# Residual tiles and norm rows loaded several steps ahead of use; a product's sums copied bank by bank in its last step

## The chip, the cores and the metric

One core of a Trainium2 chip runs the whole program. The metric is device time in microseconds (us): the median of several executions of the same program. Engines are named as in the profile: PE is TensorE's matmul, PEld its weight load, DVE is VectorE, ACT is ScalarE, POOL is GpSimd, and SP is SyncE, which here only issues DMAs (SPq is its queue).

## The reference

One layer of a decoder with 1024 tokens and width 1024, in float32. An attention and a retention branch are projected out and normalised to `x1`; then comes a gated MLP with a causal convolution of width 3 (inner width 2816). The change lies in its last lines:

```python
u = causal_depthwise_conv(h @ w_up[l], conv_w[l], conv_b[l])
a, bv = jnp.split(u, 2, axis=-1)
y = (jax.nn.gelu(a, approximate=False) * bv) @ w_down[l]
x = layer_norm(ALPHA * x + g2 * y, ln2_g[l], ln2_b[l])
```

The `x` on the right of the last line is `x1`, the result of the first sub-layer. With `g = gelu(a) * bv` as the matrix of 1024 x 2816, the stage in question computes `g @ w_down`, adds the residual `ALPHA * x1`, and normalises each row.

## The kernel before

The stages follow one another on PE: input projections, attention, retention, output projection, the up product with convolution and gate, and last the down product, on which this document centres (from 1032 us of the profile on).

**The down product** is cut 2 x 2 in each dimension and done with seven products of half size instead of eight, in the order `PORD = (1, 2, 6, 5, 3, 7, 4)` (L1379). The operands of a product `p` are sums of blocks; they lie ready in DRAM (`gd`, `sd`, `td`, and `w_down` itself), and `d_src` (L1262) says which. Each product has `NK` = 11 steps `k` over the inner dimension. A float32 operand is split into a high part `hi` (rounded to the format that PE multiplies in one pass) and the rest `lo`, and a product of two numbers takes three matmuls: hi x hi, hi x lo, lo x hi (`d_mm`, L1291). A step is 4 row tiles `i` x 3 matmuls, 128 x 128 against 128 x 512.

**Sums.** There are two sets of four banks: `X_` (products 1, 6, 7 and 4 add into it, one after the other) and `Z_` (products 2, 5 and 3; product 2 ends with new banks taken for 5). Between products the running sums are needed, so `keep` (L1368) has ACT copy the four banks to SBUF after products 1, 6 and 5 (`s1`, `u2`, `s5`), after the last matmul of all four. After product 5 it copies `Z_`, into which product 3 adds next; after product 1 and 6 it copies `X_`, which the next product does not touch. After product 7 DVE adds `X_` into `s5` (L1446), and product 4 adds into `X_` next. Product 4 runs with the row tile outside and the step inside (L1447): the first bank goes through all 11 steps before the second begins.

**Preparation.** `d_prep` (L1270) makes the operands of one step: two loads of 256 KB into a `raw` tile, issued on SP (L1273); the cast to `hi` on ACT (L1287; for product 6 two halves, L1278 and L1279); the split `lo = raw - hi` on DVE (L1288; product 6: L1280 and L1282). `d_more` (L1384) runs the preparations `AHEAD` = 11 steps before PE's step (L1381, L1409). Tiles come from tagged pools: raw tiles from `R` (4), `hi` and `lo` of even steps from `X` (16), of odd steps from `H` (16), kept tiles and residual tiles 0 to 3 from `VM` (10). A tile is free again when its last reader is done.

**Beside the products** DVE works on the result, one row tile of 128 x 1024 at a time. `finish0(i)` (L1300) takes a tile `acc`, loads `x1` rows into it (L1302), multiplies by the first norm row scaled with ALPHA (L1303) and adds the second (L1304). `result` and `part` (L1322, L1317) add the gated sums; `finish1` and `finish2` (L1334, L1350) normalise and store. `row_load(q)` (L1393) loads one of four norm rows, the same for all partitions, and for q < 2 scales it on ACT at once (L1397). They are called at fixed steps (L1412 to L1427): the two rows at product 2, steps 4 and 6; `finish0` 0 to 3 at product 6, steps 0, 2, 4, 6; 4 and 5 at product 5, steps 2 and 6; 6 and 7 at product 3, steps 2 and 6.

**Order.** Each engine and SP's queue work in order. The order is made when the program is built: instructions are taken by their place in the program, but one that is expected to be ready sooner can go first on its engine. `tc.issue_after(ins)` puts what its block issues on the engine of `ins` behind `ins`, on that engine only. Waits are put in by the framework.

Of the kernel before, what the change touches and what calls it, by code (L numbers as in the profile page):

```python
# [8 lines left out]
F32 = mybir.dt.float32  # L9
# [4 lines left out]
ALU = mybir.AluOpType  # L14
# [17 lines left out]
def kernel(  # L32
# [35 lines left out]
    def slot(tag, shape, dtype, name, padded=None):  # L68
        return gp.tile(shape, dtype, tag=tag, bufs=NB[tag], name=name, padded_shape=padded)
# [4 lines left out]
    def small(shape, name):  # L74
        return sp.tile(shape, F32, tag="s", bufs=24, name=name)

    def f(ap):
        return ap.bitcast(F32)
# [66 lines left out]
    def bcast_rows(src, n):  # L145
        return bass.AP(tensor=src.tensor, offset=src.offset, ap=[[0, P], [1, n]])
# [1112 lines left out]
    nc.sync.dma_start(g_row, bcast_rows(gates[1], D))  # L1259
    dops = {}  # L1260

    def d_src(p, k):  # L1262
        half = [slice(0, 512), slice(512, 1024)]
        a = {1: gd[2 * k, :, half[0]], 2: gd[2 * k + 1, :, half[0]], 3: sd[3, k],
             4: gd[2 * k + 1, :, half[1]], 5: sd[0, k], 6: sd[1, k], 7: sd[2, k]}[p]
        b = {1: wdq[0, k][:, half[0]], 2: wdq[1, k][:, half[0]], 3: wdq[1, k][:, half[1]],
             4: td[3, k], 5: td[0, k], 6: td[1, k], 7: td[2, k]}[p]
        return a, b

    def d_prep(p, k):  # L1270
        raw = slot("R", [P, 2, 512], F32, f"dr{p}_{k}")
        for u, src in enumerate(d_src(p, k)):
            nc.sync.dma_start(raw[:, u, :], src)  # L1273
        tag = "X" if p == 1 and k < 4 else "HX"[k % 2]
        hi = slot(tag, [P, 2, 512], F32R, f"dh{p}_{k}")
        lo = slot(tag, [P, 2, 512], F32R, f"dl{p}_{k}")
        if p == 6:
            nc.scalar.copy(hi[:, 0, :], raw[:, 0, :])  # L1278
            nc.scalar.activation(hi[:, 1, :], raw[:, 1, :], AF.Copy, scale=-1.0)  # L1279
            nc.vector.tensor_tensor(out=lo[:, 0, :], in0=raw[:, 0, :], in1=f(hi[:, 0, :]),  # L1280
                                    op=ALU.subtract)
            nc.vector.scalar_tensor_tensor(  # L1282
                out=lo[:, 1, :], in0=raw[:, 1, :], scalar=-1.0, in1=f(hi[:, 1, :]),
                op0=ALU.mult, op1=ALU.subtract,
            )
        else:
            nc.scalar.copy(hi, raw)  # L1287
            nc.vector.tensor_tensor(out=lo, in0=raw, in1=f(hi), op=ALU.subtract)  # L1288
        dops[p, k] = (hi, lo)

    def d_mm(p, k, i, pt, start, stop):  # L1291
        hi, lo = dops[p, k]
        q = slice(i * P, (i + 1) * P)
        for n_, (w_, m_) in enumerate(((hi, hi), (hi, lo), (lo, hi))):
            nc.tensor.matmul(pt, w_[:, 0, q], m_[:, 1, :], start=start and n_ == 0,  # L1295
                             stop=stop and n_ == 2, skip_group_check=True)

    lrow, fr, fin = [], [], {}

    def finish0(i):  # L1300
        acc = slot("VM" if i < 4 else "H", [P, D], F32, f"r{i}")
        nc.sync.dma_start(acc, x1d[i])  # L1302
        nc.vector.tensor_tensor(out=acc, in0=acc, in1=lrow[0], op=ALU.mult)  # L1303
        nc.vector.tensor_tensor(out=acc, in0=acc, in1=lrow[1], op=ALU.add)  # L1304
        fin[i] = [acc, small([P, 2], f"fsum{i}")]

    def gated(i, n, src, dst):

# [8 lines left out]
    def part(i, n, src):  # L1317
        sl = slice(n * 512, (n + 1) * 512)
        gated(i, n, src, src)
        nc.vector.tensor_tensor(out=fin[i][0][:, sl], in0=fin[i][0][:, sl], in1=src, op=ALU.add)  # L1320

    def result(i, n, src, dst, first):  # L1322

        acc, sums = fin[i]
        sl = slice(n * 512, (n + 1) * 512)
        gated(i, n, src, dst)
        nc.vector.tensor_tensor_reduce(
            out=acc[:, sl], in0=acc[:, sl], in1=dst, scale=1.0,
            scalar=(0.0 if first else sums[:, 0:1]),
            op0=ALU.add, op1=ALU.add,  # L1330
            accum_out=sums[:, 0:1] if first else sums[:, 1:2],
        )
# [32 lines left out]
        if i < NT - 1:  # L1365
            nc.sync.dma_start(out[i * P:(i + 1) * P, :], o)

    def keep(pts, name, tag):  # L1368

        ts = [slot(tag, [P, 2, 512], F32, f"{name}{q}") for q in range(2)]  # L1370
        for i in range(4):
            nc.scalar.copy(ts[i // 2][:, i % 2, :], pts[i])  # L1372
        return [ts[i // 2][:, i % 2, :] for i in range(4)]

    def banks4(name):
        t = [bank2(f"{name}{i}") for i in range(2)]
# [7 lines left out]
    def d_more(n):  # L1384
        nonlocal need
        while need < min(n, len(prep)):
            d_prep(*prep[need])
            need += 1

    def dscr(name):  # L1390
        return tmp([P, 512], F32, name)

    def row_load(q):  # L1393
        r_ = slot("X", [P, D], F32, f"frow{q}")
        nc.sync.dma_start(r_, bcast_rows(ln_rows[q], D))
        if q < 2:
            nc.scalar.activation(r_, r_, AF.Copy, scale=ALPHA)  # L1397
        (lrow, fr)[q // 2].append(r_)

    d_more(4)  # L1400
    X_ = [bank(f"dX{i}") for i in range(4)]
    for pi, p in enumerate(PORD[:-1]):
        on_x = p in (1, 6, 7)
        if p in (2, 5):
            Z_ = banks4(f"dZ{p}_")
        pts = X_ if on_x else Z_
        start, stop = p in (1, 2, 5), p in (2, 3)
        for k in range(NK):
            d_more(pi * NK + k + 1 + AHEAD)  # L1409
            for i in range(4):  # L1410
                d_mm(p, k, i, pts[i], start and k == 0, stop and k == NK - 1)
            if p == 2 and k in (4, 6):  # L1412
                row_load(k // 2 - 2)
            if p == 6 and k in (0, 2, 4, 6):
                finish0(k // 2)
            if p == 5:
                if k in (1, 3, 5, 7):
                    result(k // 2, 0, s1[k // 2], s1[k // 2], True)
                if k in (2, 6):
                    finish0(4 + k // 4)  # L1420
            if p == 3:
                if k in (1, 3, 5, 7):
                    part(k // 2, 1, u2[k // 2])
                if k in (2, 6):
                    finish0(6 + k // 4)
                if k in (4, 8):
                    row_load(1 + k // 4)  # L1427
        if p == 1:
            s1 = keep(X_, "ds1_", "VM")
        elif p == 2:  # L1430
            for i in range(4):
                nc.vector.tensor_tensor(out=s1[i], in0=s1[i], in1=Z_[i], op=ALU.subtract)
        elif p == 6:
            u2 = keep(X_, "du2_", "VM")
        elif p == 5:
            s5 = keep(Z_, "ds5_", "VM")
        elif p == 3:
            for i in range(4):
                result(i, 1, Z_[i], dscr(f"dt{i}"), False)
            for i in range(4):  # L1440
                if i > 0:
                    finish2(i - 1)
                finish1(i)
            finish2(3)
    for i in range(4):
        nc.vector.tensor_tensor(out=s5[i], in0=s5[i], in1=X_[i], op=ALU.add)  # L1446
    for i in range(4):  # L1447
        for k in range(NK):
            d_mm(4, k, i, X_[i], False, k == NK - 1)
# [79 lines left out]
```

## Time and profile before

| | us |
|---|---|
| median of 3 runs | 1264.28 |
| lowest and highest run | 1261.54, 1265.71 |
| the profiled execution | 1270.5 |
| its span, first to last instruction | 1268.8 |
| PE busy in it | 1226.6 |
| DVE, ACT, POOL busy | 928.2, 630.4, 247.9 |
| mean granted clock of TensorE | 0.989 of full speed |

The times of rows are from the profiled execution, counted from the first instruction. The down product begins at 1032 us (its first matmul in the regular sequence at 1035.6) and PE's last matmul ends at 1260.6; from there DVE, ACT and a store take the span to its end. Matmuls overlap, so the distance of their starts tells the pace, not the duration in the row.

### The profile page before, as it was taken

The numbers are of one execution on the slowest core, as the hardware profiler recorded it, in microseconds if no ns is written. First come the engines' busy times: TensorE is split into PE (matmuls) and PEld (weight loads), VectorE is DVE, ScalarE is ACT, GpSimd is POOL, SyncE is SP. The second block draws the span as 40 slices with busy tenths as digits, with TensorE's granted clock in tenths as the row PEclk, the third lists the DMA queues.
The fourth block names the chain that finished last, engine by engine and source line by source line (L and its number), as shares of the span: only waits on it lengthen the run. The fifth ranks groups of instructions, "written<-read, shape, count | busy, mean of one in ns | idle before, by whom it ended". The sixth has DMA issues, their size and how long they took to land.

```text
span 1268.8 us, 17244 instructions
## 1 busy us (share of the span) xinstructions
PE 1226.6 (97%) x6077; PEld 1022.3 (81%) x6077; DVE 928.2 (73%) x1774; ACT 630.4 (50%) x1144; POOL 247.9 (20%) x293
## 2 busy tenths in 40 slices
PE   6999999999999999999899999999999999998997
PEld 5788888898888887788788888888888878886876
DVE  6774685784877778747897787787787785784775
ACT  3633232333766668467764454454454565443342
POOL 0034153410433334300003222221101010000021
PEclk9999999999999999999899999999999999998989
DMA  9534152533234236222248877786544689866641
GB/s 354 206 96 137 52 155 95 168 118 118 84 96 146 76 100 195 90 98 105 79 137 211 216 179 178 199 191 159 157 133 126 181 249 278 298 214 203 209 150 67
DMA packets 86047, 199.79 MB, mean 157 GB/s; under 512 B 9861, under 2 KB 16197, under 8 KB 85961
## 3 DMA queue, kind: packets, MB, share of 16 engines
q1 hardware_dynamic: 73288, 175.62, 40.2%
q0 software_dynamic: 12672, 23.07, 11.6%
q8 instruction: 48, 0.79, 0.2%
q14 instruction: 39, 0.31, 0.1%
HBM read 165.06 MB, written 68.20 MB: 184 GB/s over the span
## 4 chain that ended last, share of the span: by engine, by line
PE 74%; DVE 11%; DMA 7%; ACT 4%; issue 2%; SPq 1%; POOL 0%; DVEq 0%; ACTq 0%; POOLq 0%
PE uX L1123 6%; PE uX L1124 6%; PE uX L1125 6%; PE dX L1295 5%; PE uY L1124 4%; PE uY L1125 4%; PE uY L1123 4%; PE rp L208 3%; PE rp L209 3%; PE rp L207 3%; PE pv L793 3%; DVE dl L1288 2%; PE dZ L1295 2%; DMA xt<-in_xT_dram 2%; PE qk L709 2%
## 5 line engine op out<-in xcount | busy, mean ns | idle before, releaser
L1287 ACT CAST dh<-dr 128x1024 fp32r<-128x1024 f32 x66 | 68.2, 1051 | 97.3 <-DMA dr<-in_w_down_dram 39.0
L1288 DVE TENSOR_TENSOR dl<-dr,dh 128x1024 fp32r<-128x1024 f32 x66 | 80.6, 1236 | 42.5 <-ACT dh L1287 32.7
L755 POOL TENSOR_TENSOR S<-S,dn 128x128 f32<-128x128 f32 (+3 forms) x64 | 74.1, 1162 | 150.4 <-DVE dn L754 97.8
L970 POOL DMA_DIRECT2D sd<-gd x22 | 18.1, 823 | 395.2 <-DMA sd<-y 233.0
L207 PE MATMUL rp<-wr,hhi 128*128 128x512 f32 x200 | 79.2, 396 | 1.3 <-ACT rst L367 1.3
L208 PE MATMUL rp<-wr,hhi 128*128 128x512 f32 x200 | 79.0, 395 | 0.1
L209 PE MATMUL rp<-wr,hlo 128*128 128x512 f32 x200 | 78.8, 394 | 0.0
L1295 PE MATMUL dX<-dh 128*128 128x512 f32 x176 | 69.8, 397 | 3.1 <-DVE ds L1446 3.1
L1295 PE MATMUL dX<-dl,dh 128*128 128x512 f32 x176 | 69.7, 396 | 0.0
L1295 PE MATMUL dX<-dh,dl 128*128 128x512 f32 x176 | 69.5, 395 | 0.0
L1138 ACT COPY u<-uX 128x512 f32<-128x512 f32 x44 | 25.8, 586 | 73.8 <-PE uX L1125 73.8
L1295 PE MATMUL dZ<-dh 128*128 128x512 f32 x132 | 52.8, 400 | 5.9 <-ACT ds L1372 5.9
L751 ACT ACTIVATE S<-S,mn 128x128 f32<-128x128 f32 (+3 forms) x64 | 49.9, 779 | 15.1 <-DVE mn L746 13.9
L709 PE MATMUL qk<-hhi,wqh 128*128 128x512 f32 x128 | 54.6, 426 | 0.0
L784 DVE TENSOR_TENSOR pt<-pt,pt 128x512 fp32r<-128x512 f32 (+2 forms) x96 | 50.8, 550 | 4.3 <-ACT pt L783 3.1
L746 DVE CUSTOM_DVE_ANT_0 S<-ps,nb 128x128 f32<-128x128 f32 (+3 forms) x64 | 47.9, 750 | 8.0 <-PE ps L744 5.6
L1295 PE MATMUL dZ<-dl,dh 128*128 128x512 f32 x132 | 52.4, 397 | 0.0
L1295 PE MATMUL dZ<-dh,dl 128*128 128x512 f32 x132 | 52.3, 398 | 0.0
L793 PE MATMUL pv<-pt,V 128*128 128x256 f32 x320 | 49.9, 293 | 2.4 <-DVE pt L784 1.2
L208 PE MATMUL op<-wol,mxs 128*128 128x512 f32 x128 | 50.4, 394 | 1.7 <-DVE wol L893 1.5
L207 PE MATMUL op<-woh,mxs 128*128 128x512 f32 x128 | 50.7, 398 | 0.9 <-DVE mn L746 0.9
L711 PE MATMUL qk<-hhi,wql 128*128 128x512 f32 x128 | 51.6, 403 | 0.0
(1058 smaller groups left out, 3833.4 us busy)
## 6 DMA issues: line engine op xcount, KB each, us to landing
ada<-in_ada_dram SPq DMA_DIRECT2D x48, 512.0 KB, 3.9
td<-in_w_down_dram SPq DMA_DIRECT2D x44, 256.0 KB, 5.5
wa<-in_w_up_dram SPq DMA_DIRECT2D x22, 512.0 KB, 5.6
wb<-in_w_up_dram SPq DMA_DIRECT2D x22, 512.0 KB, 4.0
gd<-y SPq DMA_DIRECT2D x22, 512.0 KB, 2.7
sd<-y SPq DMA_DIRECT2D x44, 256.0 KB, 3.4
dr<-sd SPq DMA_DIRECT2D x44, 256.0 KB, 4.0
dr<-td SPq DMA_DIRECT2D x44, 256.0 KB, 3.4
```

Of the source, the lines that this page charges most:

```text
L207: nc.tensor.matmul(pt, ahi, whi, start=start, stop=False)
L208: nc.tensor.matmul(pt, ahi, wlo, start=False, stop=False)
L209: nc.tensor.matmul(pt, alo, whi, start=False, stop=stop)
L709: nc.tensor.matmul(pt, whi[:, j, :], hhi[j][:, sl], start=(j == 0), stop=False)
L755: nc.gpsimd.tensor_tensor(out=Ssb[:, :span], in0=Ssb[:, :span], in1=den.to_broadcast([P, span]), op=ALU.mult,)
L793: nc.tensor.matmul(pv[:, :256], V2[h][:, kb, :], pts[kb // 4][u][:, kb % 4, :], start=(kb == 0 and u == 0), stop=(kb == nkb - 1 and u == 1),)
L1123: nc.tensor.matmul(pt, whi, bh, start=start, stop=False, skip_group_check=True)
L1124: nc.tensor.matmul(pt, whi, bl, start=False, stop=False, skip_group_check=True)
L1125: nc.tensor.matmul(pt, wlo, bh, start=False, stop=stop, skip_group_check=True)
L1287: nc.scalar.copy(hi, raw)
L1288: nc.vector.tensor_tensor(out=lo, in0=raw, in1=f(hi), op=ALU.subtract)
L1295: nc.tensor.matmul(pt, w_[:, 0, q], m_[:, 1, :], start=start and n_ == 0, stop=stop and n_ == 2, skip_group_check=True)
```

## The change

`finish0` loses its load, which becomes `rest_load`, called four to seven steps earlier. The first two rows are loaded at product 2, steps 0 and 1, and scaled by a call of its own at steps 6 and 8. `keep` now also issues the matmuls of the last step, one bank at a time, each followed by its copy. In the last three steps of product 5 no preparation is issued; the three follow after the copies, and on ACT behind the last copy. At the end of product 7 each bank's matmuls are followed by its add, and the splits of product 4's last three steps go behind the first add on DVE. The other calls of the table `SIDE` stand at the same steps as before.

```diff
+    LATE = [(4, k) for k in range(NK - 3, NK)]
+    late = []
...
         if p == 6:
             nc.scalar.copy(hi[:, 0, :], raw[:, 0, :])
             nc.scalar.activation(hi[:, 1, :], raw[:, 1, :], AF.Copy, scale=-1.0)
...
         else:
             nc.scalar.copy(hi, raw)
-            nc.vector.tensor_tensor(out=lo, in0=raw, in1=f(hi), op=ALU.subtract)
         dops[p, k] = (hi, lo)
+
+        def low():
...
+            else:
+                nc.vector.tensor_tensor(out=lo, in0=raw, in1=f(hi), op=ALU.subtract)
+
+        if (p, k) in LATE:
+            late.append(low)
+        else:
+            low()
...
-    def finish0(i):
+    def rest_load(i):
         acc = slot("VM" if i < 4 else "H", [P, D], F32, f"r{i}")
         nc.sync.dma_start(acc, x1d[i])
+        fin[i] = [acc, small([P, 2], f"fsum{i}")]
+
+    def finish0(i):
+        acc = fin[i][0]
         nc.vector.tensor_tensor(out=acc, in0=acc, in1=lrow[0], op=ALU.mult)
         nc.vector.tensor_tensor(out=acc, in0=acc, in1=lrow[1], op=ALU.add)
-        fin[i] = [acc, small([P, 2], f"fsum{i}")]
...
-    def keep(pts, name, tag):
-
-        ts = [slot(tag, [P, 2, 512], F32, f"{name}{q}") for q in range(2)]
+    def keep(p, k, pts, name):
+
+        ts = [slot("VM", [P, 2, 512], F32, f"{name}{q}") for q in range(2)]
+        ts = [ts[i // 2][:, i % 2, :] for i in range(4)]
         for i in range(4):
-            nc.scalar.copy(ts[i // 2][:, i % 2, :], pts[i])
-        return [ts[i // 2][:, i % 2, :] for i in range(4)]
+            d_mm(p, k, i, pts[i], False, False)
+            order["ACT"] = nc.scalar.copy(ts[i], pts[i])
+        return ts
...
+    SIDE = {
+        2: {0: [(row_load, 0)], 1: [(row_load, 1)], 3: [(rest_load, 0)], 5: [(rest_load, 1)],
+            7: [(rest_load, 2)], 9: [(rest_load, 3)],
+            6: [(row_scale, 0)], 8: [(row_scale, 1)]},
+        6: {0: [(finish0, 0)], 2: [(finish0, 1)], 4: [(finish0, 2)], 6: [(finish0, 3)],
+            7: [(rest_load, 4)], 9: [(rest_load, 5)]},
+        5: {1: [(first_part, 0)], 2: [(finish0, 4)], 3: [(first_part, 1)],
+            5: [(first_part, 2), (rest_load, 6)], 6: [(finish0, 5)], 7: [(first_part, 3)],
+            8: [(rest_load, 7)]},
+        3: {1: [(second_part, 0)], 2: [(finish0, 6)], 3: [(second_part, 1)],
+            4: [(row_load, 2)], 5: [(second_part, 2)], 6: [(finish0, 7)],
+            7: [(second_part, 3)], 8: [(row_load, 3)]},
+    }
...
         for k in range(NK):
-            d_more(pi * NK + k + 1 + AHEAD)
-            for i in range(4):
-                d_mm(p, k, i, pts[i], start and k == 0, stop and k == NK - 1)
...
+            if not (p == 5 and k >= NK - 3):
+                d_more(pi * NK + k + 1 + AHEAD)
+            if k == NK - 1 and p in (1, 6, 5):
+                kept = keep(p, k, pts, f"ds{p}_")
+            else:
+                for i in range(4):
+                    d_mm(p, k, i, pts[i], start and k == 0, stop and k == NK - 1)
+                    if p == 7 and k == NK - 1:
+                        add = nc.vector.tensor_tensor(
+                            out=s5[i], in0=s5[i], in1=X_[i], op=ALU.add)
+                        if i == 0:
+                            with tc.issue_after(add.ins):
+                                for low in late:
+                                    low()
+            for fn, i in SIDE.get(p, {}).get(k, ()):
+                fn(i)
...
         elif p == 5:
-            s5 = keep(Z_, "ds5_", "VM")
+            s5 = kept
+            with tc.issue_after(order["ACT"].ins):
+                d_more((pi + 1) * NK + AHEAD)
...
-    for i in range(4):
-        nc.vector.tensor_tensor(out=s5[i], in0=s5[i], in1=X_[i], op=ALU.add)
```

`first_part` and `second_part` are the calls of `result` and `part` from before under a name; `row_scale` is the scaling that stood in `row_load`.

## Rows read from the trace of the kernel before

**Rows 1.** The page, engine totals and TensorE's clock in 40 slices.

```profile
PE 1226.6 (97%) x6077; PEld 1022.3 (81%) x6077; DVE 928.2 (73%) x1774; ACT 630.4 (50%) x1144; POOL 247.9 (20%) x293
...
PEclk9999999999999999999899999999999999998989
```

**Rows 2.** Waits of PE, whole span: total us, times, longest.

```profile
PE m L232 <- DMA ada<-in_ada_dram: 7.5, 1, 7.5
PE dZ L1295 <- ACT ds L1372: 5.9, 2, 3.9
PE dX L1295 <- DVE ds L1446: 3.1, 1, 3.1
```

**Rows 3.** Table by stretches: us, busy PE PEld DVE ACT POOL, clock, DMA share, GB/s.

```profile
1065.30:1095.20 29.90, 29.90 (x133) 24.77 (x132) 17.10 (x24) 18.80 (x31) 0.00 (x0) 1.00 0.91 310
1095.20:1125.20 30.00, 30.00 (x134) 24.83 (x133) 29.85 (x38) 13.08 (x13) 0.00 (x0) 1.00 0.69 240
...
1155.07:1194.40 39.33, 33.41 (x134) 26.92 (x134) 18.38 (x16) 14.35 (x16) 0.00 (x0) 0.91 0.61 206
1194.40:1224.30 29.90, 29.90 (x133) 24.57 (x131) 28.42 (x38) 18.29 (x26) 6.46 (x4) 1.00 0.61 214
1224.30:1260.70 36.40, 33.23 (x133) 26.76 (x132) 20.79 (x40) 8.88 (x14) 3.88 (x3) 0.91 0.12 49
```

**Rows 4.** Chain that ended last, from 860 us: start, us, what.

```profile
1035.78 29.69 PE dX L1295 x131
...
1227.55 33.09 PE dX L1295 x132
```

**Rows 5.** Timeline of PE around product 3's start: start, us, operation.

```profile
1154.84 0.39 PE L1295 MATMUL dZ<-dh,dl 128*128 128x512 f32 x1
...
1160.18 0.63 PE L1295 MATMUL dZ<-dh,dl 128*128 128x512 f32 x1
...
1160.61 0.63 PE L1295 MATMUL dZ<-dh 128*128 128x512 f32 x1
```

**Rows 6.** Chain that ended last, 1143 to 1166 us.

```profile
1144.41 5.92 DMA r<-x1d
...
1153.10 2.95 DMA dr<-td
...
1156.15 1.05 ACT dh L1287
...
1163.42 1.08 ACT ds L1372 x2
```

**Rows 7.** Timeline of ACT: start, us, line, operation, idle before and releaser.

```profile
1130.98 2.04 ACT L1372 COPY du<-dX 128x512 f32<-128x512 f32 x4
...
1224.50 1.04 ACT L1287 CAST dh<-dr 128x1024 fp32r<-128x1024 f32 x1 [4.20 <-DMA dr<-td]
```

**Rows 8.** Timeline of DVE around the end of product 7.

```profile
1225.58 1.23 DVE L1288 TENSOR_TENSOR dl<-dr,dh 128x1024 fp32r<-128x1024 f32 x1 [1.67 <-ACT dh L1287]
1226.72 1.28 DVE L1446 TENSOR_TENSOR ds<-ds,dX 128x512 f32<-128x512 f32 x2
...
1229.71 1.22 DVE L1288 TENSOR_TENSOR dl<-dr,dh 128x1024 fp32r<-128x1024 f32 x1
```

**Rows 9.** Waits of DVE, 1025 to 1269 us: total us, times, longest.

```profile
DVE r L1303 <- DMA r<-x1d: 9.3, 2, 5.3
```

**Rows 10.** Waits of ACT, 1025 to 1269 us.

```profile
ACT dh L1287 <- PE dZ L1295: 10.3, 7, 2.2
...
ACT frow L1397 <- DMA frow<-in_ln_rows_dram: 3.3, 2, 2.6
```

**Rows 11.** Raw loads L1273, 1140 to 1160 us: issue to landing.

```profile
DMA to landing us min/median/max: 2.7/3.2/6.4
```

**Rows 12.** Timeline of DVE in product 2.

```profile
1069.44 1.22 DVE L1288 TENSOR_TENSOR dl<-dr,dh 128x1024 fp32r<-128x1024 f32 x1 [1.24 <-ACT dh L1287]
```

More of the change, by code (lines that the diff above doesn't have):

```diff
@@ L1279, in d_prep @@
             nc.scalar.activation(hi[:, 1, :], raw[:, 1, :], AF.Copy, scale=-1.0)
[L1280 to L1285, printed above, removed]
         else:
             nc.scalar.copy(hi, raw)
-            nc.vector.tensor_tensor(out=lo, in0=raw, in1=f(hi), op=ALU.subtract)
         dops[p, k] = (hi, lo)
+        def low():
+            if p == 6:
+                nc.vector.tensor_tensor(out=lo[:, 0, :], in0=raw[:, 0, :], in1=f(hi[:, 0, :]),
+                                        op=ALU.subtract)
+                nc.vector.scalar_tensor_tensor(
+                    out=lo[:, 1, :], in0=raw[:, 1, :], scalar=-1.0, in1=f(hi[:, 1, :]),
+                    op0=ALU.mult, op1=ALU.subtract,
+                )
+            else:
[4 more added lines that the diff above has]
+            low()
     def d_mm(p, k, i, pt, start, stop):
@@ L1391, in dscr, with row_scale, first_part, second_part @@
         return tmp([P, 512], F32, name)
+    rows_ = []
     def row_load(q):
[L1394 to L1398, printed above, removed]
+        rows_.append(slot("X", [P, D], F32, f"frow{q}"))
+        nc.sync.dma_start(rows_[q], bcast_rows(ln_rows[q], D))
+        (lrow, fr)[q // 2].append(rows_[q])
+    def row_scale(q):
+        nc.scalar.activation(rows_[q], rows_[q], AF.Copy, scale=ALPHA)
+    def first_part(i):
+        result(i, 0, s1[i], s1[i], True)
+    def second_part(i):
+        part(i, 1, u2[i])
+    SIDE = {
[11 more added lines that the diff above has]
+    }
     d_more(4)
@@ L1408 @@
         for k in range(NK):
-            d_more(pi * NK + k + 1 + AHEAD)
-            for i in range(4):
-                d_mm(p, k, i, pts[i], start and k == 0, stop and k == NK - 1)
[L1412 to L1427, printed above, removed]
+            if not (p == 5 and k >= NK - 3):
[14 more added lines that the diff above has]
+                fn(i)
         if p == 1:
-            s1 = keep(X_, "ds1_", "VM")
+            s1 = kept
         elif p == 2:
@@ L1433 @@
         elif p == 6:
-            u2 = keep(X_, "du2_", "VM")
+            u2 = kept
         elif p == 5:
-            s5 = keep(Z_, "ds5_", "VM")
+            s5 = kept
+            with tc.issue_after(order["ACT"].ins):
+                d_more((pi + 1) * NK + AHEAD)
         elif p == 3:
```

## The prediction

> **What bounds the kernel now.** I read the page first: TensorE (PE) is busy for 97% of the span and its granted clock is full nearly everywhere [rows 1]. So time can only come from places where PE stands still or runs at the lower of its two clock levels, and only in the stage that the diff edits, the seven down products in the order 1, 2, 6, 5, 3, 7, 4. The list of waits comes next. In that stage PE waits for two things: 5.9 us in two waits on the copies of L1372, 3.1 us in one wait on the adds of L1446 [rows 2]. The longest wait of the kernel, 7.5 us on a load at the start, is not touched.
>
> Third, the table by stretches, cut at the products' borders [rows 3]. In the two stretches shown from 1065.30 to 1125.20 (products 2 and 6) PE is busy throughout at granted clock 1.00, as it is in product 7 (1194.40 to 1224.30). The two stretches with a clock of 0.91 are product 3, entered through the first wait, and product 4, entered through the second.
>
> The clean pace is in the chain of waits: 131 matmuls in 29.69 us, 0.2266 us each [rows 4]. A step of a product is 12 matmuls, 2.72 us; a product of 11 steps takes 29.9 us. After the first wait the starts are 0.43 us apart (1160.18, 1160.61) [rows 5], the pace of the 1.2 GHz level. So each wait costs its idle time and then a stretch of slow matmuls:
> - products 3 and 7 last 39.33 + 29.90 = 69.2 us [rows 3]; 264 matmuls at the clean pace are 59.8. Lost: 9.4, of which 5.9 are idle and 3.5 slow.
> - product 4 takes 33.1 us for 132 matmuls [rows 4], 3.0 more than 131 x 0.2266 + 0.39 for the last. Before it lies the 3.25 us between 1224.30 and 1227.55. Lost: 6.25.
>
> Together 15.6 us, the most that taking both waits away can give.
>
> **Why they are there.** ACT, DVE and SP each work through their own queue in order. The chain that ends in the first wait [rows 6]: a residual load (r<-x1d) takes 5.92 us; DVE stands in front of L1303 for it, so a split queued behind (L1288) frees its raw tile late; SP can then issue the next raw load only at 1153.10; its cast on ACT starts at 1156.15; and the copies that PE needs are queued behind casts, the last pair at 1163.42, because one more cast was put between the two pairs. Product 5's last matmul had started at 1154.84 [rows 5]: ACT held its sums up, not the copying. Four copies in a row take 2.04 us [rows 7].
>
> The second wait: DVE's add starts at 1226.72, right behind the split that began at 1225.58, whose cast began at 1224.50 after a DMA wait of 4.20 us [rows 7, 8]. The add had nothing to wait for but PE, done by 1224.30.
>
> **The change, part by part.**
> *Copies bank by bank* (products 1, 6, 5). No copy is added. Bank 0 has its last matmul nine matmuls, 2.04 us, before the product ends. With ACT free, copies of 0.5 us at bank intervals of 0.68 us keep up, and the last is done about 0.8 us after the product's end. Product 3 comes to bank 3 only 9 x 0.2266 = 2.04 us after its start, so PE waits for none. In products 1 and 6 PE does not use the copied banks in the next product; worth nothing there, hidden by a PE that is 100% busy.
> *Three preparations held back.* In product 5, steps 8 to 10 prepare nothing; the three go behind the last copy: 3 casts of 1.05 and 3 splits of 1.23 us [rows 6, 8], with six loads of 256 KB on SP. The loads are not held by the added order, only by the four raw tiles. The preparations are those of product 3's steps 8 to 10, needed 8 steps, 21.8 us, after its start; three casts and three splits take about 6 us after the copies. Hidden, with 15 us to spare; without that cover it is 3 x 2.72 = 8.2 us of lead.
> *Adds and three late splits* (end of product 7). The first add (0.64 us) can start 2 us before PE needs it; the three splits go behind it, 3.7 us, ending about 2.5 us after product 7. Product 4 needs steps 8, 9, 10 at 5.4, 6.1 and 6.8 us after its start. Even before, with the adds in between, the last of these splits ended at 1229.71 + 1.22 = 1230.93 [rows 8], 6.6 us after 1224.30. It fits, narrowly.
> *Residual and row loads earlier.* The same eight residual loads and four row loads, no byte more. DVE loses 9.3 us of waiting in two waits [rows 9], ACT 3.3 us in two [rows 10]. None of it is on PE's path directly; it removes the cause at the head of [rows 6]. What is late next there is the ordinary raw load, 3.2 us median to landing [rows 11]. The two row scalings move behind loads that landed steps before: nothing. Buffers: residual tiles 4 to 7 hold an H tile up to six steps longer; 16 less 4 leaves 12, six odd steps, so the look-ahead of 11 steps still fits. X keeps 14 beside the two early rows.
> *SP's queue.* In product 2 now come four residual loads of 0.5 MB beside the two row loads, so at most 2 MB more than before: at 310 GB/s 6.8 us of transfer, into a stretch whose DMA share is already 0.91 of 29.90 us [rows 3]. At most 4 us stay uncovered by free DMA time. The cover is the lead: the last split of product 2 started at 1069.44 [rows 12], 4 us into a product whose step 10 PE reaches at 1065.3 + 27.2 = 1092.5. So I cost it at nothing; if that lead were gone it would be 4 us of waiting.
>
> Here the Trainium skill speaks against the change: DMA: Bandwidth & Descriptors, section "Queues, rings and completion order", says that each DMA engine takes descriptors in ring order, so a large load issued early on SP's queue goes ahead of the small ones behind it. By that rule the raw loads behind each moved load would be late, a rival below; the trace agrees, since raw loads took up to 6.4 us around a residual load against 3.2 [rows 11].
>
> **Sum.** The profiled execution took 1270.5 us (span 1268.8, 1.7 around it). Less 15.6: 1254.9. It stands 6.2 above the median of the runs, 1264.28. The trace cannot say where the runs are shorter. If all 6.2 are in these two waits, the gain in the runs is 9.4 (1254.9); if none, 15.6 (1248.7). I take a third of it in them, as another wait of 7.5 us hangs on loads too [rows 2] and most of the span lies outside this stage: gain about 13.5, **1251 us**.
>
> **Rivals.**
> - *The copies still queue behind a cast* (the change doesn't do what it says for the first wait). The code orders the three held-back preparations behind the copies, not the one after them, which needs only the fourth raw tile. If its load is late, ACT stands as in [rows 6]. Only the second wait goes: 1264.3 - 6.25 = 1258. Against: its raw tile is freed steps earlier once DVE does not stand for residuals. Chance 0.12.
> - *Early loads push raw loads back* (product 2): 4 us of waiting plus 3 us of slow matmuls, with both old waits gone: 1251 + 7 = 1258. Against: the lead of [rows 12]. Chance 0.08.
> - *Preparation becomes the bound and nothing comes of it.* If loads, casts and splits do not move forward with PE, product 7 ends 9.4 us earlier, at 1214.9, and its step 10 falls due 6.8 later, 1221.7, against a split that ends at 1230.93: 9.2 us of waiting and 3 slow, leaving 3.4: 1261. For: raw loads hold ACT often. Against: seven waits of ACT, 10.3 us, were for PE to give tiles back [rows 10], so the preparations were ahead of PE. Chance 0.13.
> - *Slower: the held-back preparations are never made up.* Place: entry to product 4, which eats 11 steps of tiles in 7.5 us. With lead L at the end of product 7 and one preparation per 2.72 us, step 10 is ready (11 - L) x 2.72 us later, due at 6.8. The old loss of 15.6 is matched at about 12.6 us of waiting plus 3 slow, which is 19.4 us, L below 4. With L = 3 it is 15 + 3 + 1.5 slow: 1268. Against: DVE was idle for 39.33 - 18.38 = 21 us in product 3 [rows 3], room to catch up. Chance 0.07.
>
> **Numbers.** The forecast has 0.60; its own range is 1246 (full gain and the 2.7 us by which the fastest run undercuts the median) to 1255. The two rivals at 1258 lie inside the range and the one at 1261 is near its upper end, so 1246 to 1262 leaves out the slower one and tails. A change within 0.3%, 3.8 us, cannot be told from none. Faster: 0.60 + 0.12 + 0.08 = 0.80. Same: 0.13. Slower: 0.07.
>
> **What would show it.** Right: no PE wait on the copies or above 0.5 us on the adds; granted clock 1.00 from product 1 into product 4; products 3, 7 and 4 at 29.9 us each; no DVE wait on x1d; the copies of product 5 starting before its last matmul, in a row or at 0.7 us steps. Wrong: a cast between the copies of product 5 (first rival); a PE wait on tiles in product 2 or 6 (second); a PE wait on a split within the first bank of product 4 (third, fourth). A gain well over 16 us would mean that time came from outside this stage.

## The result, and the profile after

The changed kernel takes **1254.85 us** (median of 4 runs, 1253.71 to 1255.73), the kernel before 1263.11 beside it (4 runs, 1261.54 to 1265.71): ratio 0.9932, 95% interval 0.9911 to 0.9953, so 6 to 11 us faster. The forecast was 1251, its range 1246 to 1262. The profiled execution takes 1255.27 us with a span of 1253.5, against 1270.5 and 1268.8 before.

Engine totals and TensorE's granted clock on the page of the changed kernel (answers to [rows 1]):

```profile
PE 1220.3 (97%) x6077; PEld 1017.6 (81%) x6077; DVE 929.4 (74%) x1774; ACT 630.9 (50%) x1144; POOL 247.9 (20%) x293
...
PEclk9999999999999999999999999999999999999999
```

The number of instructions is the same on every engine, and the two 8s near the right end of the clock line, where the two waits were, are gone. The third 8, near 620 us, stands in a stage that the change does not touch, and it went only because the slices fall elsewhere: from 590 to 640 us the granted clock is 0.93 in both kernels. Next the waits of PE from 1030 us to the end (total us, times, longest), to be held against [rows 2]:

```profile
PE uX L1123 <- DVE ub L1161: 0.5, 1, 0.5
```

Neither the copies nor the adds are in the list. The line that is left stands in front of the first down product and was there before. The chain that ended last (start, us, what), answering to [rows 4]:

```profile
1035.53 29.69 PE dX L1307 x131
1065.22 29.92 PE dZ L1307 x132
1095.14 29.92 PE dX L1307 x132
1125.06 60.42 PE dZ L1307 x264
1185.48 59.85 PE dX L1307 x264
...
1245.36 0.70 DVE dt L1326
```

From the first down product to the last the chain is PE alone. In the kernel before, the same chain went through DMA, DVE and ACT. Every product takes 29.9 us, but for products 5 and 3 together: 60.42 is 0.6 more than 264 matmuls at 0.2266 us. The table by stretches (us, busy PE PEld DVE ACT POOL, clock, DMA share, GB/s; products 2, 3, 7 and 4) answers to [rows 3]:

```profile
1065.10:1095.00 29.90, 29.90 (x134) 24.75 (x133) 24.91 (x31) 20.39 (x32) 0.00 (x0) 1.00 0.97 350
...
1154.90:1185.30 30.40, 30.40 (x134) 24.89 (x133) 15.95 (x14) 15.12 (x16) 0.00 (x0) 1.00 0.76 259
1185.30:1215.20 29.90, 29.90 (x133) 24.77 (x132) 27.95 (x38) 18.19 (x26) 6.46 (x4) 1.00 0.59 202
1215.20:1245.30 30.10, 30.10 (x133) 24.59 (x132) 21.21 (x39) 8.88 (x14) 3.87 (x3) 1.00 0.14 55
```

The clock is 1.00 in all of them, where products 3 and 4 had 0.91. The first line shows product 2 with the early loads: 350 GB/s at a DMA share of 0.97, and PE still busy all the time. In the same stretch of the other profiles the kernels with early loads have 342 to 352 GB/s, those with the old ones 310 to 338.

Why the first wait went is in the timeline of ACT around product 5's end (1155.27, half of the 60.42 us after 1125.06):

```profile
1152.98 1.26 ACT L1389 COPY ds<-dZ 128x512 f32<-128x512 f32 x2 [9.84 <-PE dZ L1307]
1154.63 1.28 ACT L1389 COPY ds<-dZ 128x512 f32<-128x512 f32 x2 [0.39 <-PE dZ L1307]
1155.81 3.89 ACT L1284 CAST dh<-dr 128x1024 fp32r<-128x1024 f32 x4
```

ACT has stood idle for 9.84 us when PE hands it the first bank; four copies in a row, no cast among them, and the last ends at 1155.91, 0.64 us after the product. Before, two casts stood in front of the copies and one between the pairs, the first and the last of them held up by a load:

```profile
1156.15 1.99 ACT L1287 CAST dh<-dr 128x1024 fp32r<-128x1024 f32 x2 [7.79 <-DMA dr<-td]
1158.04 1.07 ACT L1372 COPY ds<-dZ 128x512 f32<-128x512 f32 x2
1162.47 1.04 ACT L1287 CAST dh<-dr 128x1024 fp32r<-128x1024 f32 x1 [3.36 <-DMA dr<-td]
```

Both late loads are from `td`. Product 3 does not read it and product 7 does, so ACT stood in front of operands that PE needs only a product later.

And the second wait, in the timeline of DVE around product 7's end (1215.4, half of the last chain entry):

```profile
1211.38 2.35 DVE L1296 TENSOR_TENSOR dl<-dr,dh 128x1024 fp32r<-128x1024 f32 x2
1213.65 0.68 DVE L1459 TENSOR_TENSOR ds<-ds,dX 128x512 f32<-128x512 f32 x1
1216.49 1.23 DVE L1296 TENSOR_TENSOR dl<-dr,dh 128x1024 fp32r<-128x1024 f32 x1 [2.16 <-ACT dh L1284]
1217.63 0.68 DVE L1459 TENSOR_TENSOR ds<-ds,dX 128x512 f32<-128x512 f32 x1
1218.23 2.36 DVE L1296 TENSOR_TENSOR dl<-dr,dh 128x1024 fp32r<-128x1024 f32 x2
```

The first add starts at 1213.65, 1.8 us before the product's end. The splits behind it still wait 2.16 us for a cast, but now it is the second add, not the first, that stands behind that wait; the last split ends at about 1220.6, 5.2 us into product 4, which needs it at 6.8.

### The profile page after: what moved, and what is told of

The parts are those of the page before. It is cut to its first block, busy times and chain, and to the rows that moved or that the text cites. A ratio compares the mean times of both kernels' runs of the same rounds, so it can differ in the third digit from the quotient of the medians.

```text
span 1253.5 us, 17244 instructions
## 1 busy us (share of the span) xinstructions
PE 1220.3 (97%) x6077; PEld 1017.6 (81%) x6077; DVE 929.4 (74%) x1774; ACT 630.9 (50%) x1144; POOL 247.9 (20%) x293
## 3 DMA queue, kind: packets, MB, share of 16 engines
q0 software_dynamic: 12672, 23.07, 11.6%
## 4 chain that ended last, share of the span: by engine, by line
PE 85%; DVE 7%; ACT 3%; DMA 3%; issue 1%; SPq 0%; POOL 0%; DVEq 0%; ACTq 0%; POOLq 0%
PE dX L1307 10%; PE dZ L1307 7%; PE uX L1123 6%; PE uX L1124 6%; PE uX L1125 6%; PE uY L1125 4%; PE uY L1124 4%; PE uY L1123 4%; PE rp L208 3%; PE rp L209 3%; PE rp L207 3%; PE pv L793 3%; DMA xt<-in_xT_dram 2%; PE qk L709 2%; PE qk L710 2%; PE qk L711 2%
```

## One measure for all runs

The start of the first down product moves by up to 2.6 us from profile to profile (1033.16 to 1035.78), which has nothing to do with the change. So each profile is also read as **the stretch from there to the end of the span**: 1268.8 - 1035.78 = 233.0 us before, 1253.5 - 1035.53 = 218.0 after. In the table "first" and "second" are PE's waits on the copies of product 5 and on the adds of product 7. Stretch and waits belong to one execution, the profiled one, whose own time is given beside them: where the runs spread widely it can stand well off the median.

| run | what it is | median us (lowest to highest, runs) | ratio to before, 95% interval | profiled us | stretch us | first, second wait us |
|---|---|---|---|---|---|---|
| before | shown ahead of the prediction | | | 1270.5 | 233.0 | 5.9, 3.1 |
| after | all of the change | 1254.85 (1253.71 to 1255.73, 4) | 0.9932 [0.9911, 0.9953] | 1255.27 | 218.0 | 0, 0 |
| e1 | kernel before, again | 1265.03 (1262.15 to 1269.49, 12) | 0.9998 [0.9981, 1.0015] | 1263.83 | 226.8 | 1.9, 4.3 |
| e2 | after, loads as before | 1254.78 (1253.41 to 1254.99, 5) | 0.9907 [0.9885, 0.9929] | 1253.41 | 218.0 | 0, 0 |
| e3 | after, copies and preparations as before | 1255.71 (1253.29 to 1261.76, 6) | 0.9921 [0.9893, 0.9949] | 1255.52 | 219.5 | 1.7, 0 |
| e4 | after, adds and splits as before | 1259.18 (1257.91 to 1260.38, 6) | 0.9944 [0.9924, 0.9964] | 1260.38 | 223.1 | 0, 3.3 |
| e5 | after, again | 1253.48 (1253.09 to 1254.50, 6) | 0.9917 [0.9899, 0.9934] | 1253.25 | 218.0 | 0, 0 |
| e6 | before, with the adds and late splits | 1260.14 (1256.16 to 1263.63, 12) | 0.9972 [0.9956, 0.9988] | 1256.16 | 221.5 | 1.9, 0 |
| e7 | before, with the copies and held-back preparations | 1260.19 (1259.01 to 1261.40, 12) | 0.9968 [0.9956, 0.9980] | 1261.40 | 224.6 | 0, 5.0 |
| e8 | after, splits not late | 1258.52 (1257.28 to 1259.77, 7) | 0.9959 [0.9940, 0.9978] | 1257.99 | 223.1 | 0, 3.2 |
| e9 | after, preparations not held back | 1260.35 (1253.66 to 1264.08, 12) | 0.9960 [0.9941, 0.9980] | 1258.91 | 222.8 | 3.4, 0 |
| e10 | after, copies behind all matmuls | 1253.81 (1253.02 to 1255.41, 6) | 0.9919 [0.9899, 0.9939] | 1253.30 | 217.5 | 0, 0 |
| e11 | before, with the early loads | 1259.26 (1257.80 to 1267.92, 12) | 0.9976 [0.9955, 0.9996] | 1257.80 | 221.9 | 0.4, 2.0 |
| e12 | before, with the two edits of order | 1253.37 (1252.83 to 1253.77, 6) | 0.9913 [0.9894, 0.9933] | 1253.41 | 217.5 | 0, 0 |

e1 to e4, e5 to e8 and e9 to e12 each ran on one chip, beside runs of the kernel before with a median of 1265.12, 1262.48 and 1263.43 us. So medians are compared within a group.

## The experiments

**e1: the kernel before, unchanged.** Is what the trace of before showed the same each time?

> The kernel before, unchanged, profiled a second time and timed against itself. Theory (the two waits vary from one execution to the next, and the first profile caught long ones): ratio 1.000, runs of 1262 to 1265 us, and this profile shows less than 9.0 us for the two waits together, with an own time nearer to the runs than 1270.5. Rival (being profiled lengthens the waits each time): about 9 us of waits again and an own time of 1268 to 1271, 5 us or more above the runs.

Its waits of PE (total us, times, longest):

```profile
PE dX L1295 <- DVE ds L1446: 4.3, 1, 4.3
PE dZ L1295 <- ACT ds L1372: 1.9, 1, 1.9
```

The same two waits, 6.2 us instead of 9.0, and shared out the other way, in an execution of 1263.83 us: as the theory said. The stretch is 226.8 us instead of 233.0. So the two profiles of one program differ by 6.2 us in this stretch, out of 1270.5 - 1263.83 = 6.67 in all. The runs of before spread over some 9 us.

**e2: the loads put back.** The residual tile is loaded in `finish0` again, and the rows at their old steps:

```diff
     def finish0(i):
+        rest_load(i)
-        2: {0: [(row_load, 0)], 1: [(row_load, 1)], 3: [(rest_load, 0)], 5: [(rest_load, 1)],
-            7: [(rest_load, 2)], 9: [(rest_load, 3)],
-            6: [(row_scale, 0)], 8: [(row_scale, 1)]},
+        2: {4: [(row_load, 0), (row_scale, 0)], 6: [(row_load, 1), (row_scale, 1)]},
```

> The changed kernel with the residual and row loads back at their old steps; bank-by-bank copies, held-back preparations and interleaved adds stay. Theory (the order on ACT and DVE is the whole cure): no wait of PE on the copies or adds above 0.5 us, 1253 to 1256 us, the same as the changed kernel. Rival (the residual load at the head of the chain is the cause, as the prediction put it): the wait on the copies comes back with 2 to 6 us, 1258 to 1262 us.

Measured 1254.78 and a stretch of 218.0, the same as the changed kernel, with no wait of PE. DVE waits for the residual loads longer here than in any other profile (13.2 us in 5 waits; 8.4 to 12.8 in the others), and PE waits for nothing. With the two orders in place the early loads are worth nothing that these runs can tell.

**e3: the copies as before, and nothing held back.**

```diff
-            if not (p == 5 and k >= NK - 3):
-                d_more(pi * NK + k + 1 + AHEAD)
+            d_more(pi * NK + k + 1 + AHEAD)
-            with tc.issue_after(order["ACT"].ins):
-                d_more((pi + 1) * NK + AHEAD)
         for i in range(4):
             d_mm(p, k, i, pts[i], False, False)
+        for i in range(4):
             order["ACT"] = nc.scalar.copy(ts[i], pts[i])
```

> The changed kernel with the copies after all matmuls again and no preparation held back; early loads and interleaved adds stay. Theory (order): casts stand before and between the copies, PE waits 2 to 6 us for them, and with the slow matmuls the time is 4 to 9 us above the changed kernel: 1259 to 1263 us. Rival (early loads are the cure): PE waits 1 us or less, 1255 to 1256 us.

Measured 1255.71, below what the theory expected and inside the rival's band, with runs from 1253.29 to 1261.76. The wait of 1.7 us in the profile fits neither (2 to 6, or 1 at most). ACT's timeline shows where the wait is from:

```profile
1153.45 1.04 ACT L1284 CAST dh<-dr 128x1024 fp32r<-128x1024 f32 x1 [9.44 <-DMA dr<-td]
1154.40 1.07 ACT L1390 COPY ds<-dZ 128x512 f32<-128x512 f32 x2
1155.36 1.06 ACT L1284 CAST dh<-dr 128x1024 fp32r<-128x1024 f32 x1
1156.31 1.09 ACT L1390 COPY ds<-dZ 128x512 f32<-128x512 f32 x2
```

ACT stands 9.44 us in front of a cast whose raw tile is not there, with PE's sums ready behind it. In the order of the built program that cast is the one of product 7, step 1 (its load is from `td` again): product 7 starts at 1185.76 in e3, so its tile is not needed for another 30 us. The mechanism is the predicted one. Its price here is less than expected, and from e3 alone the early loads could as well be the cure.

**e4: the adds and splits as before.**

```diff
-    LATE = [(4, k) for k in range(NK - 3, NK)]
+    LATE = []
-                    if p == 7 and k == NK - 1:
-                        add = nc.vector.tensor_tensor(
-                            out=s5[i], in0=s5[i], in1=X_[i], op=ALU.add)
...
+    for i in range(4):
+        nc.vector.tensor_tensor(out=s5[i], in0=s5[i], in1=X_[i], op=ALU.add)
     for i in range(4):
         for k in range(NK):
             d_mm(4, k, i, X_[i], False, k == NK - 1)
```

> The changed kernel with the four adds after product 7 again, in front of them all splits of product 4. Theory: one wait of PE on the adds of about 3 us and product 4 with some 3 us of slow matmuls, 4 to 6 us above the changed kernel: 1258 to 1261 us. Rival (DVE now runs ahead, as the first wait is gone and the loads are early, and the adds find it free): a wait of under 1 us, 1255 to 1256 us.

Measured 1259.18; the stretch is 5.1 us longer than after's, and the second wait is back:

```profile
PE dX L1307 <- DVE ds L1480: 3.3, 1, 3.3
```

As the theory said.

**e5: the changed kernel again**, on the chip of e6 to e8.

> The changed kernel, unchanged, on the same chip as the next three. Theory: no wait of PE on copies or adds, 1253 to 1256 us, 8 to 11 us under the kernel before, and its runs spread over less (about 2 us) than those of the kernel before (about 9 us), because what varied were the two waits. Rival (the spread is the chip's, not the waits'): its runs spread as widely as those of the kernel before.

Measured 1253.48 against 1262.48, 9.0 us less. Its 6 runs lie within 1.4 us; the 24 of the kernel before beside them spread over 9.9.

**e6: the kernel before with the adds and late splits alone** (the edits of e2 and e3 taken together).

> The kernel before with only the order at the end of product 7 changed (adds, and three splits behind the first). Theory (the second wait is the larger part in the runs): the wait on the adds is gone, one on the copies of 2 to 6 us stays, 1256 to 1260 us. Rival (the two waits share one slack, so that a wait that is taken away at one place is met at the other): PE still loses about 6 us, 1262 to 1265 us.

**e7: the kernel before with the copies and held-back preparations alone** (the edits of e2 and e4).

> The kernel before with only the copies bank by bank and three preparations held back. Theory of separate waits: the wait on the copies is gone, the one on the adds stays at 3 to 4 us, 1258 to 1261 us. Rival (shared slack: PE comes earlier to the end of product 7 and waits there for splits that do not come earlier): the wait on the adds grows to 6 us or more and the time stays at 1262 to 1265 us.

The waits of PE in e6, then in e7:

```profile
PE dZ L1307 <- ACT ds L1391: 1.9, 1, 1.9
```

```profile
PE dX L1307 <- DVE ds L1477: 5.0, 1, 5.0
```

Each half removes its own wait and leaves the other. Each alone gains only 2.3 us in the medians (1262.48 less 1260.14, less 1260.19), and both together 9.0. By the ratios it is 0.28% and 0.32% against 0.83%, and with these intervals the halves can still add up to the whole. Two things stand against reading more into it. The profile of e6 is its fastest run, 4 us under its median. And e7 is more than a half: DVE's timeline there has five splits in front of the adds, not four, the last two (1215.13 and 1217.83) each behind a wait for its cast (1.64 and 1.48 us), and the adds start only at 1218.97. So its wait of 5.0 us is partly an order that neither before nor e4 and e8 have. Whether a shorter first wait by itself makes the second longer is not shown: before and e1 have 5.9 and 3.1, 1.9 and 4.3, but e4 and e8, with early loads and no first wait, have 3.3 and 3.2.

**e8: the adds bank by bank, but the splits not late.**

```diff
-    LATE = [(4, k) for k in range(NK - 3, NK)]
+    LATE = []
```

> The changed kernel with the adds bank by bank, but no split put behind the first add. Theory (the order on DVE decides, and without the instruction the splits of steps 8 and 9 still stand in front of the adds): the wait on the adds is back with 3 to 4 us, 1258 to 1261 us, as with the old adds. Rival (issuing each add right behind its bank's matmuls is what helps): no such wait, 1254 to 1256 us.

Measured 1258.52, a wait of 3.2 us. DVE's timeline:

```profile
1209.29 3.48 DVE L1296 TENSOR_TENSOR dl<-dr,dh 128x1024 fp32r<-128x1024 f32 x3
1214.29 1.23 DVE L1296 TENSOR_TENSOR dl<-dr,dh 128x1024 fp32r<-128x1024 f32 x1 [1.52 <-ACT dh L1284]
1215.43 1.28 DVE L1459 TENSOR_TENSOR ds<-ds,dX 128x512 f32<-128x512 f32 x2
```

The adds start behind four splits, the last of which waits for its cast. Where the adds stand in the text changed nothing: around the adds DVE runs e8's instructions in the order of e4 (there too three splits, one that waits 1.64 us for its cast, and then the adds). The order given to the splits does it.

**e9: the copies bank by bank, but the preparations not held back** (e3's edit without the loop line at its end).

> The changed kernel with the copies bank by bank, but the three preparations after product 5 no longer held back. The built program then has the casts of tiles (3,9), (3,8) and (7,1) ahead of the first copy on ACT and the cast (3,10) ahead of the last. Theory (the order on ACT's queue makes the first wait, above all the cast (7,1), whose raw tile is loaded late): TensorE waits again at product 5 to 3, 1 to 3 us, 1255 to 1259 us. Rival (copying bank by bank is enough, since each copy starts 5 to 7 us earlier): no wait over 1 us, 1253 to 1255 us.

Measured 1260.35, more than the theory expected, with runs from 1253.66 to 1264.08 and a wait of 3.4 us. The chain that ended last in e9, where it leaves PE (start, us, what):

```profile
1148.47 0.65 DVE dl L1296
...
1149.51 4.76 DMA dr<-td
...
1154.36 1.04 ACT dh L1284
1155.40 0.50 ACT ds L1389
...
1155.94 6.26 PE dZ L1307 x19
```

A split frees a raw tile, its load takes 4.76 us, ACT has idled 9.55 us in front of the cast, and the copy comes last. No residual load is in this chain, though one was issued beside that raw load, at 1149.98. Copying bank by bank does not help while a cast stands in front.

**e10: the preparations held back, but the copies written behind all matmuls of the product, as before** (the loop line at the end of e3's edit alone).

> The changed kernel with the preparations held back, but the four copies written behind all 44 matmuls as before. The built program then has the same order on ACT as the changed kernel: four copies in a row, no cast among them. Theory (the order on ACT is all, where the copies stand in the text is nothing): as the changed kernel, 1253 to 1255 us, no wait over 0.5 us at product 5 to 3. Rival (bank by bank matters in itself): a wait of 1 to 1.5 us there, 1255 to 1257 us.

**e11: the kernel before with the early loads alone** (the edits of e3 and e4).

> The kernel before with the early loads alone; copies, preparations, adds and splits as before. Theory (early loads shorten the first wait, because the raw tile of (7,1) comes sooner, and leave the second at 3 to 5 us): 1258 to 1262 us, first wait under 3 us. Rival (the loads do nothing): as the kernel before, ratio 0.998 to 1.002, waits of 6 to 9 us together.

e11's median of 1259.26 is in the theory's band, 4.2 us under the kernel before, but the interval reaches to 0.9996, so a gain from the loads alone is just clear of noise and its size is not. The profile, its fastest run, has waits of 0.4 and 2.0 us, the second shorter than the theory's 3 to 5, and the runs go from 1257.80 to 1267.92.

**e12: the kernel before with two edits of order**: the preparations behind the copies of product 5, the three splits (kept in `late`, as in the change) behind the first add of product 7. Loads, copies and adds stand in the text where they stood.

```diff
+            if not (p == 5 and k >= NK - 3):
+                d_more(pi * NK + k + 1 + AHEAD)
...
+            with tc.issue_after(order["ACT"].ins):
+                d_more((pi + 1) * NK + AHEAD)
...
     for i in range(4):
-        nc.vector.tensor_tensor(out=s5[i], in0=s5[i], in1=X_[i], op=ALU.add)
+        add = nc.vector.tensor_tensor(out=s5[i], in0=s5[i], in1=X_[i], op=ALU.add)
+        if i == 0:
+            with tc.issue_after(add.ins):
+                for low in late:
+                    low()
```

> The kernel before with two edits of order alone: the three preparations behind the copies of product 5, and the three splits behind the first add of product 7. Loads, copies and adds stand where they stood. Theory (these two edits are the whole gain): as the changed kernel, 1253 to 1255 us, neither wait left. Rival (early loads or bank by bank copies carry part of it): 1256 us or more, with 1 to 4 us of a wait left.

The chain that ended last over products 5, 3, 7 and 4, in e10 and then in e12:

```profile
1123.56 59.93 PE dZ L1307 x264
1183.49 59.89 PE dX L1307 x264
```

```profile
1123.61 59.95 PE dZ L1307 x264
1183.55 59.85 PE dX L1307 x264
```

No wait in either, 1253.81 and 1253.37 us, ratios 0.9919 and 0.9913 beside the 0.9917 of e5. The two edits of order are the whole gain. And products 5 and 3 take 59.95 us where the copies are written behind the matmuls, 60.42 in the changed kernel: in the three profiles that have the copies bank by bank with no wait (after, e2, e5) the stretch is 218.0, in e10 and e12 it is 217.5. Half a microsecond is too little to see in the medians. In e10 the copies started before product 5's end too:

```profile
1152.16 1.07 ACT L1390 COPY ds<-dZ 128x512 f32<-128x512 f32 x2 [13.75 <-PE dZ L1307]
```

The product ends there at about 1153.5. Written behind all matmuls, the copies go in pairs, the first when the second bank of its pair is done, 1.3 us before the product's end; in the changed kernel the first bank's copy starts 2.3 us before it. The last copy ends 1.1 us after the product in e10 and 0.64 after it in the changed kernel, and PE waits for neither. So copies start before the product is done, wherever they are written, if nothing stands in front of them on ACT.

## Why the prediction was right, and where it was not

**What bounds it, and the two waits: right.** PE's two waits and the slow matmuls behind them were the whole of it. In the profiled executions the sum predicted 15.6 us; measured are 1270.5 - 1255.27 = 15.2, of which 15.0 lie in the stretch from the first down product. The sum needed only that both waits go, by whichever edit. For the first wait the prediction had the early loads remove the cause, and to the held-back preparations, which do it (e10, e12), it gave no gain of their own. That this edit was part of the change is luck as far as the forecast goes.

**The mis-sized term: the share of the 6.2 us.** The profiled execution stood 6.2 above the median of the runs, and I took a third of that in the two waits, since another wait of PE hangs on loads too. e1 shows where it lay: two profiles of the same program, 6.67 us apart, and 6.2 of it between the first down product and the end. So all of it belonged to the two waits and the slow matmuls behind them, the case that the prediction gave as its lower bound of the gain: 9.4 us, 1254.9. Measured 1254.85. The gain in the medians is 8.3 us here and 9.0 in e5's group, where the forecast had 13.5. The profiled execution had been one of the longer ones, and a wait that hangs on the landing of one load is the first place to look for why.

Only 2.8 of these 6.2 us are idle time: the two waits together are 9.0 us before and 6.2 in e1. The rest is slow matmuls, and here the prediction's step from each wait to a stretch of slow matmuls was too simple. In e1 the granted clock behind the first wait of 1.9 us is 1.00 (1158.50 to 1188.10); in e6, behind a first wait of the same 1.9 us, it is 0.57, mostly the lower level, from 1156.40 to 1160.00. What tells the two apart these runs do not show.

**Copies bank by bank: the effect right, the reason wrong.** The last copy ends 0.64 us after the product (0.8 predicted). But e9 and e10 show that it is the holding back that does it: the bank-by-bank text without it leaves the wait (3.4 us), and with it the old place of the copies will do.

**Held-back preparations hidden: right.** The row of four casts that follows the copies ends at 1159.70, and the four splits behind them at 1161.53, 6.3 us after the product's end, with product 3's step 8 due 21.8 us in. Nothing was late.

**Adds and late splits fit narrowly: right, but for when they end.** I had the last split 2.5 us after product 7; it ends 5.2 after, because a split still waits 2.16 us for a cast. The due time of 6.8 holds.

**Early loads: this step failed.** I wrote that DVE loses its 9.3 us of waits and that this removes the cause at the head of [rows 6]; no wait of DVE on x1d was to be a sign of being right. The waits of DVE on residual loads in the changed kernel:

```profile
DVE r L1319 <- DMA r<-x1d: 10.9, 4, 5.5
```

They are still there: 8.6 to 11.6 us in the eight profiles with early loads, 8.4 to 13.2 in the six with the old ones. The loads and the multiplies that use them, before (issues of L1302, starts of L1303) and after (L1314, L1319), with counts and first and last start:

```profile
L1302 SPq DMA_DIRECT2D r<-x1d x8: 319/422/431, 1088.6 to 1183.7; - x8
...
L1303 DVE TENSOR_TENSOR r<-r,frow x8: 1214/1217/1227, 1094.3 to 1189.4; 128x1024 f32<-128x1024 f32 x8
```

```profile
L1314 SPq DMA_DIRECT2D r<-x1d x8: 319/426/432, 1071.5 to 1144.8; - x8
...
L1319 DVE TENSOR_TENSOR r<-r,frow x8: 1219/1222/1226, 1078.4 to 1151.6; 128x1024 f32<-128x1024 f32 x8
```

The first load moved from 1088.6 to 1071.5 and the first multiply from 1094.3 to 1078.4; the last pair likewise. Written eight steps later than the load, the multiply was still put 6.9 us behind it (5.7 before). The order on DVE is not that of the text, and moving the load moved its use along. (By the table `SIDE` the residual loads stand six to nine steps ahead of their use, not four to seven, and tiles 4 to 7 would be held up to nine steps longer, not six; it did not matter, as the use came along.) ACT's wait on the norm rows did shrink, from 3.3 to 0.9 us (1.6 to 3.3 with the old loads, 0.2 to 1.8 with the early ones), worth nothing to PE.

**The cause at the head of the chain: only one of several.** Taking the residual load for the cause was too narrow. It does stand in the chain of the first wait in all three profiles that have the old loads and casts in front of the copies (before, e1, e6), and in none of the three with early loads (e3, e9, e11); but their first waits are 1.7, 3.4 and 0.4 us, not nothing. In e9 the raw load is late with no residual load in the chain; in e12 DVE waits 11.5 us for residual loads, and PE for nothing. What decides is what stands in front of the copies on ACT's queue, not why it is late on a given run.

**The rivals.** The cast between the copies did not come to pass in the changed kernel, but e3, e9 and e6 are that rival built: 1255.7 to 1260.4, where 1258 was given. That early loads push raw loads back: in product 2 the raw loads' median to landing went from 4.6 and 4.5 us to 4.9 and 5.1, and ACT's waits on them there from 6.3 to 6.8; small, and covered by the lead: the last split of product 2 starts at 1068.95, 3.7 us into the product, where it was 4 before [rows 12]. The Trainium skill's rule (DMA: Bandwidth & Descriptors, "Queues, rings and completion order") points the same way, but e2, with the old loads, has 4.7 and 4.8, so the trace does not tell its effect from that of the run. Preparation as the bound, and held-back preparations never made up: PE waits for no tile of the down product in any of the profiles, so both are out.

**What stays open** is what the early loads do while a cast still stands in front of the copies. With the copies as before, e3 has 1255.71 where e6, without the early loads, has 1260.14 (in another group; ratios 0.9921 and 0.9972), and e11 gains some 4 us over the kernel before by the loads alone. The early loads change the built order on ACT: in e6, as before, the casts of product 7, step 1, and product 3, step 10, stand in front of the copies and one of product 7, step 3, between the pairs; in e3 the first stands in front, the second between the pairs, the third behind. But e9, with the same casts in front of the first copy as e3, has 1260.35. With runs that spread over 7 to 10 us, these numbers don't settle it.

## What to carry to other kernels

Where an engine works through one queue in order, look in the order of the built program for what stands directly in front of the instruction that the bottleneck waits for; if that is preparation which is due only many microseconds later, a few lines that fix the order are worth more than loads moved ahead (here they are the whole 9 to 10 us; the loads add nothing to them, and alone bring some 4 us in the medians, with an interval that comes close to none). Moving a load earlier in the text does not make it early if its use is free to move with it: compare the times from issue to use, not the steps. And before the gain is counted against a profiled execution that stands above the median, ask first whether the wait about to be removed is what varies, and profile the kernel before a second time.

## What was not expected of the hardware

**The spread of the runs sorts the kernels.** Where a cast of a raw tile not yet loaded stands in front of product 5's copies, the runs spread over 7 to 11 us: 7.3 (e1), 9.9 (before, beside e5), 8.5 (e3), 7.5 (e6), 10.4 (e9), 10.1 (e11); only the 4 runs of before beside the result lie within 4.2. Where it does not, over 0.9 to 2.5: after 2.0, e2 1.6, e4 2.5, e5 1.4, e7 2.4, e8 2.5, e10 2.4, e12 0.9. e7 and e6 have 12 runs each, so it is not their number. The second wait, alone in e4, e7 and e8, costs 3 to 5 us and leaves the spread at 2.5. The raw load in question took 2.95 us in [rows 6] and 4.76 in e9, and the moment at which it could be issued moved as well. That this load is what varies from run to run is an argument from one profile of each kernel.

**Copies written between the banks cost PE a little.** With them, four of PE's matmuls between 1153.23 and 1155.61, at the border of products 5 and 3, start 0.34 to 0.39 us after the one before instead of 0.2266, at a granted clock of 1.00; that is the half microsecond between 60.42 and 59.95. It is not the copying beside the matmuls as such, since copies run before the product's end in e10 too. That the four extra signals to ACT are the reason is an argument, not a measurement.
